# The first tiles of a streaming-encoder layer in another order: input tiles and weights by pairs, squares and the first gate's norm later

## The chip, the cores and the metric

The kernel runs on one core of a Trainium2 chip. The metric is the device time of one execution in microseconds (us). The engines named below are PE (TensorE: matmuls), ACT (ScalarE), DVE (VectorE), POOL (GpSimd) and SP (the engine that issues most transfers); each works through its own queue of instructions in a fixed order, and semaphores make one wait for another.

## What is computed

One layer on 528 tokens (512 of the input, 16 learned ones ahead of them) of width 1024: a half-weight SwiGLU feed-forward block, a mixing block of two head groups side by side, and a second half-weight SwiGLU block; each reads an RMS-normed stream and adds to it.

```python
def rmsnorm(x, g):
    y = xf * lax.rsqrt(jnp.mean(xf * xf, axis=-1, keepdims=True) + NORM_EPS)
    return (y * g.astype(jnp.float32)).astype(x.dtype)

def swiglu(x, w_gate, w_up, w_down):
    return (jax.nn.silu(x @ w_gate) * (x @ w_up)) @ w_down

#  h += 1/2 * SwiGLU(RMSNorm(h))                     feed-forward 1
#  n = RMSNorm(h); z = n @ W_in
#  h += concat(rwkv_out, attn_out) @ W_out           mixing: 8 RWKV heads, 8 windowed attention heads
#  h += 1/2 * SwiGLU(RMSNorm(h))                     feed-forward 2, then a final RMSNorm
```

The change touches the start of feed-forward 1. Everything else is the same work.

## The kernel before

**Numbers.** All is float32. A float32 operand is split into a rounded part (hi) and the rest (lo), both in the format that PE reads, and a product is made of three matmuls: weight hi by token hi (line 218), weight hi by token lo (line 219), and weight lo by token hi (line 200). 

**Tokens and units.** The tokens stand in two halves, half A (hf 0, 272 tokens) and half B (hf 1, 256). Weights come in units of 128 x 1024, eight blocks of 128 x 128 (k-tiles) each. Feed-forward 1 of half A runs unit by unit: gate of column block 0, up of block 0, gate of 1, up of 1 and so on; I number these units 0, 1, 2, 3. A unit is 16 hi matmuls and 8 lo matmuls in one PSUM bank; the tag `big` has four banks. `prep` (line 116) brings a unit: SP starts the transfer of `raw`, ACT casts it to `whi` (CAST, line 124), DVE subtracts to get `wlo` (line 127), each with three buffers. `drive` (line 133) keeps three units ahead of the one that is being multiplied.

**The start.** `consts0` (line 230) loads the small table `pv` of gains and runs 12 warm-up matmuls on a tile of ones (line 239). The first unit alone is brought in two halves of four k-tiles, each followed by `load_x`, four k-tiles of the input of half A. `boot[0]` = `start2(0)` then makes the norm of half A: squares on ACT (line 306), added up on DVE (line 310), summed over partitions by a matmul with ones (line 315), a square root on ACT (line 319, behind a load of its function table) and a reciprocal on DVE (line 320). Its result, `rs`, isn't needed for the operands of half A: `split` (line 331) makes them as input times gain (ACT, line 346: `nh`; DVE, line 347: `nl`), and `rs` comes in only behind the matmuls, in `up` (lines 381 to 404): gate bank times `rs` (DVE, line 396; this frees the gate's bank), silu (ACT, line 397, a function of another table), times `rs` (line 398), times the up bank (line 401; this frees the up bank), and the split of the product into hi and lo (lines 402 and 403). `ahead` makes all eight operands of half A at once. Half B's squares and norm (`start2(1)`) stand in the program behind step 22; its operands (`n1a`, `n1b`) do need `rs`.

**What sets the order.** The program is written step by step, but a scheduler that simulates the engines' time lines sets the order in each engine's queue. So an edit at the start can move rows far away from it. Names in the queues carry running numbers.

**Near the end of the mixing of half B** attention is interleaved with units of feed-forward 2 of half A. For each group of heads there are scores (line 907), a softmax on DVE and ACT (lines 913 to 923), transposes of it on PE into the banks `as` (lines 934 and 936), copies `pT` by ACT (lines 941 and 943), and products with the values (lines 946 and 949). There is one pair of `as` banks.

Of the kernel before, what the change touches and what calls it, by code (L numbers as in the profile page):

```python
# [7 lines left out]
F32 = mybir.dt.float32  # L8
R = mybir.dt.float32r
AF = mybir.ActivationFunctionType  # L10
ALU = mybir.AluOpType
# [14 lines left out]
T0 = (0, 272)  # L26
TT = (272, 256)
# [11 lines left out]
NK = D // 128  # L39
# [8 lines left out]
NPC = _n  # L48
# [7 lines left out]
UNIT = {}  # L56
# [14 lines left out]
class Prog:  # L71
# [44 lines left out]
    def prep(self, key, nk, first=False):  # L116
        raw = self.t(self.wp, [128, NK, 128], "raw", bufs=RAWB)
        hi = self.t(self.wp, [128, NK, 128], "whi", R, bufs=HIB)
        lo = self.t(self.wp, [128, NK, 128], "wlo", R, bufs=LOB)
        n = nk // 2 if first else nk  # L120
        for a in range(0, nk, n):
            self.nc.sync.dma_start(out=raw[:, a:a + n].rearrange("p k c -> p (k c)"),
                                   in_=self.io["w"][UNIT[key], :, a * 128:(a + n) * 128])
            self.A.copy(out=hi[:, a:a + n], in_=raw[:, a:a + n])  # L124
            if first:
                self.load_x(0, a)
        self.V.tensor_tensor(out=lo[:, 0:nk], in0=raw[:, 0:nk], in1=hi[:, 0:nk].bitcast(F32), op=ALU.subtract)  # L127
        return hi, lo

# [98 lines left out]


    def consts0(self):  # L230
        self.pv = self._ld("pv", [128, NPC])
# [55 lines left out]
        return self.dv[:, DC[name] + i:DC[name] + i + 1]  # L287


    def load_x(self, hf, d):  # L290
# [6 lines left out]
        self.nc.sync.dma_start(out=self.resv[:, d:d + 4], in_=self.io["xT"][:, d:d + 4, T0[hf]:T0[hf] + T])  # L297

    def sq_acc(self, hf, d, c0, end=False):

# [27 lines left out]

        return [self.t(self.np_, [128, 4, 2, T], f"n{hf}{x}", R) for x in "ab"]

    def split(self, hf, gain, c0, rs=None, ahead=True):

        T = TT[hf]
        parts = {}
        tiles = self.operands(hf, T)

        def part(d):
            if d in parts:
                return parts[d]
            np_ = tiles[d // 4][:, d % 4]  # L340
            nh, nl = np_[:, 0], np_[:, 1]
            n = self.res[hf, d]
            if rs is not None:
# [17 lines left out]
    def ffn_gu(self, f, g, hfs, ns):  # L361

        steps = []
        c0 = {hf: RO[hf] if f == 2 else 0 for hf in hfs}
        W = {hf: TT[hf] - c0[hf] for hf in hfs}
        j0, j1 = GROUPS[f][g]
        st = {}
        wide = f == 2 and tuple(hfs) == (1,)

        def gate(w):  # L370
            if wide:
                b = self.bank()
                self.wide3(b, w, ns[1], range(NK), 0, NK - 1)
                st["g"] = {1: self.both(b, self.t(self.fin, [128, 256], "gs", bufs=2))}
                return
            st["g"] = {hf: self.bank() for hf in hfs}
            self.mm3([st["g"][hf][:, :W[hf]] for hf in hfs], w, [ns[hf] for hf in hfs], NK)

        def up(j):
            def f_(w):  # L380
                pg, pu = st["g"], {hf: self.bank() for hf in hfs}
                if wide:
                    self.wide3(pu[1], w, ns[1], range(NK), 0, NK - 1)
                    pu = {1: self.both(pu[1], self.t(self.fin, [128, 256], "us", bufs=2))}
                else:
                    self.mm3([pu[hf][:, :W[hf]] for hf in hfs], w, [ns[hf] for hf in hfs], NK)
                for hf in hfs:
                    n = W[hf]
                    sl, hx = (self.sl[1], 1) if hf != hfs[0] else (self.sl[0], 0)
                    h = self.t(sl, [128, 2, TT[0]], f"h{hx}{j - j0}", R)  # L390
                    h = h.rearrange("p a t -> p (a t)")[:, 0:2 * n].rearrange("p (a t) -> p a t", a=2)
                    hh, hl = h[:, 0], h[:, 1]
                    s = self.t(self.tp, [128, TT[0]], "silu", bufs=2)
                    if f == 1 and hf == 0:
                        rs = self.rs1[hf]
                        self.V.tensor_tensor(out=s[:, :n], in0=pg[hf][:, :n], in1=rs[:, :n], op=ALU.mult)
                        self.A.activation(s[:, :n], s[:, :n], AF.Silu)
                        self.V.tensor_tensor(out=s[:, :n], in0=s[:, :n], in1=rs[:, :n], op=ALU.mult)
                    else:
                        self.A.activation(s[:, :n], pg[hf][:, :n], AF.Silu)  # L400
                    self.V.tensor_tensor(out=s[:, :n], in0=pu[hf][:, :n], in1=s[:, :n], op=ALU.mult)
                    self.A.copy(out=hh[:, :n], in_=s[:, :n])
                    self.V.tensor_tensor(out=hl[:, :n], in0=s[:, :n], in1=hh[:, :n].bitcast(F32), op=ALU.subtract)
                    self.hs[f, g, hf, j - j0] = h
# [553 lines left out]
def program(tc, io, out):  # L958
    with ExitStack() as ctx:
        pr = Prog(ctx, tc, io)  # L960
        n = {}
        A, B, AB = (0,), (1,), (0, 1)

        def renorm(gain, f):
            def last(hf):
                n[hf] = pr.norm(hf, gain, RO[hf] if f == 2 else 0)
            return last
# [21 lines left out]
        act = lambda fn: [(None, 0, 0, fn)]  # L989
# [7 lines left out]
        def pclose(name):  # L997
            pools.pop(name)[0].__exit__(None, None, None)

        def start2(hf):  # L1000
            def f():
                for d in range(NK):
                    pr.sq_acc(hf, d, 0)
                pr.rs1[hf] = pr.rstd(hf, 0, pr.mbank())
            return f

# [67 lines left out]
        fa = ffn(2, range(len(GROUPS[2])), A, final)  # L1074
        k = 10
# [6 lines left out]
        def lazy(hf):  # L1082
            made = []

            def n_(k):
                if not made:
                    made.append(pr.split(hf, "f1", 0, pr.rs1[hf] if hf else None, hf == 0))
                return made[0](k)
            return n_

        for hf in AB:
            n[hf] = lazy(hf)
        pr.drive(steps)
        pclose("fin")

# [111 lines left out]
```

## Time and profile before

| | us |
|---|---|
| median of three runs (1125.13 to 1130.59) | 1125.61 |
| the profiled execution | 1126.56 |
| its span, first to last instruction | 1124.5 |
| PE busy in the span | 1080.1 (96%) |
| DVE busy | 824.9 (73%) |
| ACT busy | 675.3 (60%) |
| POOL busy | 36.1 (3%) |

The profiled execution stands 0.95 us above the median of the runs, and 2.06 us of it lie outside the span. A line of the time line of an engine reads: start, duration, engine, line and operation, output <- inputs with shapes, number of instructions in the group, and in brackets how long the engine was idle just before and what released it. A line of a table by stretches reads: stretch, its length, then for each engine busy time and number of instructions, then PEclk, the share of full speed at which PE's clock was granted, the DMA share and GB/s.

### The profile page before, as it was taken

How to read it: one execution, taken by the hardware profiler on the slowest of the kernel's cores; microseconds unless marked ns; L12 is line 12 of the kernel's file. 1: busy time of each engine (PE TensorE's matmuls, PEld its weight loads, DVE VectorE, ACT ScalarE, POOL GpSimd, SP SyncE). 2: the span in 40 equal slices, each digit the busy share in tenths (PEclk: the TensorE clock that was granted, in tenths of full speed). 3: DMA queues.
4: the chain of work that ended last, by engine and by line, in shares of the span. 5: the costliest groups of instructions: out<-in, count | busy, mean ns of one | idle time of the engine just before them, and what ended most of it. 6: DMA issues, size and time to landing. Idle time of an engine off the chain costs nothing.

```text
span 1124.5 us, 23829 instructions
## 1 busy us (share of the span) xinstructions
PE 1080.1 (96%) x9621; PEld 1016.9 (90%) x9621; DVE 824.9 (73%) x1533; ACT 675.3 (60%) x1167; POOL 36.1 (3%) x91
## 2 busy tenths in 40 slices
PE   8999999999999997999999999998998999999996
PEld 7999999999899997988999898997887998888884
DVE  7866565777678995467799677996467588766666
ACT  7544444677666743587668685563577467545453
POOL 0000000022000000000002000000000000000000
PEclk8999999999999998999999999998999899999998
DMA  7556655655346546333555446547234456666561
GB/s 264 189 172 185 188 177 162 187 150 167 116 130 176 170 127 196 96 91 105 172 175 170 134 133 173 152 150 191 96 96 129 134 171 202 202 208 189 185 194 56
DMA packets 68721, 178.81 MB, mean 159 GB/s; under 512 B 21620, under 2 KB 26868, under 8 KB 68612
## 3 DMA queue, kind: packets, MB, share of 16 engines
q1 hardware_dynamic: 52384, 173.70, 50.3%
q10 hardware_dynamic: 16228, 3.61, 1.6%
q8 instruction: 75, 1.23, 0.4%
q14 instruction: 34, 0.28, 0.1%
HBM read 173.54 MB, written 3.74 MB: 158 GB/s over the span
## 4 chain that ended last, share of the span: by engine, by line
PE 72%; DVE 13%; ACT 7%; issue 3%; DMA 3%; ACTq 1%; DVEq 0%; SPq 0%
PE big L218 17%; PE big L219 16%; PE big L200 12%; PE big L206 11%; PE big L208 5%; DVE wlo L127 4%; PE big L227 4%; DVE tmp L731 3%; DVE rn L733 2%; ACT whi L124 2%; DMA zk<-d 1%; DMA d<-GT 1%; ACT s L920 1%; ACT L400 1%; DVE res L446 1%
## 5 line engine op out<-in xcount | busy, mean ns | idle before, releaser
L124 ACT CAST whi<-raw 128x1024 fp32r<-128x1024 f32 (+1 forms) x321 | 334.8, 1045 | 291.3 <-PE big L219 145.4
L127 DVE TENSOR_TENSOR wlo<-raw,whi 128x1024 fp32r<-128x1024 f32 x320 | 389.3, 1218 | 104.6 <-ACT whi L124 84.2
L219 PE MATMUL big<-h,whi 128*128 128x256 f32 (+1 forms) x528 | 135.4, 289 | 0.0
L218 PE MATMUL big<-h,whi 128*128 128x256 f32 (+1 forms) x528 | 131.9, 288 | 0.9 <-ACT silu L400 0.9
L218 PE MATMUL big<-n0a,whi 128*128 128x272 f32 (+1 forms) x464 | 122.3, 293 | 4.3 <-ACT n0a L346 2.3
L219 PE MATMUL big<-n0a,whi 128*128 128x272 f32 (+1 forms) x464 | 120.6, 289 | 0.4 <-DVE n0a L347 0.3
L218 PE MATMUL big<-n0b,whi 128*128 128x272 f32 (+1 forms) x464 | 120.4, 290 | 0.4 <-ACT n0b L346 0.3
L219 PE MATMUL big<-n0b,whi 128*128 128x272 f32 (+1 forms) x464 | 120.1, 289 | 0.4 <-DVE n0b L347 0.4
L219 PEld LDWEIGHTS big<-h,whi 128*128 128x128 f32 x528 | 101.1, 192 | 1.6 <-issue 1.3
L218 PEld LDWEIGHTS big<-h,whi 128*128 128x128 f32 x528 | 100.4, 193 | 1.3 <-ACT silu L400 1.1
L218 PEld LDWEIGHTS big<-n0a,whi 128*128 128x128 f32 x464 | 88.1, 190 | 6.8 <-ACT n0a L346 2.5
L219 PEld LDWEIGHTS big<-n0b,whi 128*128 128x128 f32 x464 | 88.1, 190 | 2.0 <-DVE n0b L347 0.7
L219 PEld LDWEIGHTS big<-n0a,whi 128*128 128x128 f32 x464 | 88.3, 191 | 1.6 <-DVE n0a L347 0.9
L218 PEld LDWEIGHTS big<-n0b,whi 128*128 128x128 f32 x464 | 88.0, 191 | 1.5 <-ACT n0b L346 0.9
L218 PE MATMUL big<-n1a,whi 128*128 128x256 f32 x288 | 76.2, 294 | 7.9 <-ACT whi L124 6.0
L227 PE MATMUL big<-h,wlo 128*128 128x256 f32 (+1 forms) x528 | 80.1, 286 | 0.3 <-DVE wlo L127 0.3
L200 PE MATMUL big<-n0a,wlo 128*128 128x272 f32 (+1 forms) x464 | 75.8, 285 | 0.0
L200 PE MATMUL big<-n0b,wlo 128*128 128x272 f32 (+1 forms) x464 | 75.7, 284 | 0.0
L219 PE MATMUL big<-n1a,whi 128*128 128x256 f32 x288 | 74.4, 288 | 0.0
L218 PE MATMUL big<-n1b,whi 128*128 128x256 f32 x288 | 73.9, 289 | 0.4 <-ACT n1b L953 0.4
L219 PE MATMUL big<-n1b,whi 128*128 128x256 f32 x288 | 73.9, 288 | 0.0
L227 PEld LDWEIGHTS big<-h,wlo 128*128 128x128 f32 x528 | 70.1, 188 | 2.2 <-issue 1.1
(313 smaller groups left out, 2216.1 us busy)
## 6 DMA issues: line engine op xcount, KB each, us to landing
raw<-w_in SPq DMA_DIRECT2D x319, 512.0 KB, 3.7
outT<-o SPq DMA_DIRECT2D x8, 256.0 KB, 2.6
res<-xT_in SPq DMA_DIRECT2D x2, 544.0 KB, 5.3
res<-xT_in SPq DMA_DIRECT2D x2, 512.0 KB, 9.0
d<-GT ACTq DMA_DIRECT2D x8, 80.0 KB, 4.2
zk<-d ACTq DMA_DIRECT2D x2, 320.0 KB, 4.1
d<-rn ACTq DMA_DIRECT2D x2, 320.0 KB, 3.9
GT<-d ACTq DMA_DIRECT2D x8, 80.0 KB, 5.1
```

The costliest lines, as they stand in the source:

```text
L124: self.A.copy(out=hi[:, a:a + n], in_=raw[:, a:a + n])
L127: self.V.tensor_tensor(out=lo[:, 0:nk], in0=raw[:, 0:nk], in1=hi[:, 0:nk].bitcast(F32), op=ALU.subtract)
L200: self.PE.matmul(o, lo[:, k], x(k)[:, 0], start=False, stop=(k == ks[-1]))
L206: self.PE.matmul(o, hi[:, i], x(k).rearrange("p a t -> p (a t)"), start=(k == first), stop=False)
L208: self.PE.matmul(o[:, 0:256], lo[:, i], x(k)[:, 0], start=False, stop=(k == last))
L218: self.PE.matmul(o, w, x[:, 0], start=first, stop=False)
L219: self.PE.matmul(o, w, x[:, 1], start=False, stop=False)
L227: self.PE.matmul(o, lo[:, i], x(k)[:, 0], start=False, stop=(k == nk - 1))
L400: self.A.activation(s[:, :n], pg[hf][:, :n], AF.Silu)
L446: self.V.scalar_tensor_tensor(out=r, in0=ps[hf][:, :W[hf]], scalar=0.5, in1=r, op0=ALU.mult, op1=ALU.add)
L731: V.tensor_tensor(out=m, in0=NT[:n2, 0:k, k].unsqueeze(1).broadcast_to([n2, k, k]), in1=TI[:n2, 0:k, 0:k], op=ALU.mult)
L733: V.tensor_reduce(out=TI[:n2, 0:k, k], in_=m, op=ALU.add, axis=mybir.AxisListType.X)
```

## The change

It has five parts.

1. **Order of the first transfers.** The input of half A is brought by two k-tiles instead of four. SP's order is: input 0 to 1, weights 0 to 3, `pv`, input 2 to 3, input 4 to 5, input 6 to 7, weights 4 to 7.
2. **The first cast by pairs.** ACT casts the first unit in four steps of two k-tiles (128 x 256); behind each step the operands of these two k-tiles are asked for (`first_x`).
3. **Two operands change their engine.** The hi part of k-tiles 6 and 7 of half A is made by DVE (a TENSOR_SCALAR, line 362 of the new kernel) instead of ACT (`turn`).
4. **Squares and norm of half A later.** The squares become a step behind unit 0, and `rs` of half A is made when the first gate's hidden product first asks for it.
5. **The first hidden product a unit later.** For column block 0 of half A the chain gate x `rs`, silu, x `rs`, x up is put off by one step (`self.late`): it is written behind the gate of block 1.

```diff
     def prep(self, key, nk, first=False):
-        n = nk // 2 if first else nk
+        n = 2 if first else nk
+        if first:
+            dma = lambda a, b: self.nc.sync.dma_start(out=raw[:, a:b]..., in_=self.io["w"][UNIT[key], :, a * 128:b * 128])
+            self.load_x(0, 0, 2)
+            dma(0, 4)
+            self.pv = self._ld("pv", [128, NPC])
+            for d in (2, 4, 6):
+                self.load_x(0, d, 2)
+            dma(4, 8)
+        else:
+            self.nc.sync.dma_start(out=raw[:, 0:n]..., in_=self.io["w"][UNIT[key], :, 0:n * 128])
         for a in range(0, nk, n):
-            self.nc.sync.dma_start(out=raw[:, a:a + n]..., in_=self.io["w"][UNIT[key], :, a * 128:(a + n) * 128])
             self.A.copy(out=hi[:, a:a + n], in_=raw[:, a:a + n])
             if first:
-                self.load_x(0, a)
+                for d in (a, a + 1):
+                    self.first_x(d)
...
-            self.A.activation(nh[:, c0:T], n[:, c0:T], AF.Copy, scale=self.P_(gain, d))
+            if d in turn:
+                self.V.tensor_scalar(out=nh[:, c0:T], in0=n[:, c0:T], scalar1=self.P_(gain, d), scalar2=0.0,
+                                     op0=ALU.mult, op1=ALU.add)
+            else:
+                self.A.activation(nh[:, c0:T], n[:, c0:T], AF.Copy, scale=self.P_(gain, d))
...
                     if f == 1 and hf == 0:
-                        rs = self.rs1[hf]
+                            if hf not in self.rs1:
+                                self.rs1[hf] = self.rstd(hf, 0, self.mbank())
+                            rs = self.rs1[hf]
...
+                if f == 1 and j == 0 and hfs == (0,):
+                    self.late.append((0, hidden))
+                else:
+                    hidden()
...
-        pr.boot = {0: start2(0), 2: load_b}
+        pr.boot = {2: load_b}
-        steps = fa[:22] + act(start2(1)) + fa[22:26]
+        steps = fa[:1] + act(lambda: squares(0)) + fa[1:22] + act(start2(1)) + fa[22:26]
...
-                    made.append(pr.split(hf, "f1", 0, pr.rs1[hf] if hf else None, hf == 0))
+                    made.append(pr.split(hf, "f1", 0, pr.rs1[hf] if hf else None, False, () if hf else (6, 7)))
```

In the queues the change shows at the following places. **SP, from its first transfer on**; `res` is the input, `raw` the weights. Before:

```order
1 L280 DMA pv<-pv_in 128x84
2 L122 DMA raw_100<-w_in 128x512
3 L297 DMA res_105<-xT_in 128x4x272
4 L122 DMA raw_100<-w_in 128x512
5 L297 DMA res_105<-xT_in 128x4x272
6 L122 DMA raw_138<-w_in 128x1024
```

Now:

```order
1 L308 DMA res_101<-xT_in 128x2x272
2 L123 DMA raw_98<-w_in 128x512
3 L291 DMA pv<-pv_in 128x84
4 L308 DMA res_101<-xT_in 128x2x272 x3
5 L123 DMA raw_98<-w_in 128x512
6 L132 DMA raw_133<-w_in 128x1024
```

The first input pair has moved to the front, and the second half of the first unit's weights behind all of the input; from row 6 on the queue is the same.

**ACT, where the square root of half A's norm stands.** `sq` are squares of half B, `whi_154` of before and `whi_149` of now are both the cast of unit 3, and `acc_5` / `acc_17` the square root of half A. Before:

```order
20 L306 ACTIVATE sq_938<-res_150 128x256
21 L306 ACTIVATE sq_941<-res_150 128x256
22 L124 CAST whi_154<-raw_153 128x1024
23 L306 ACTIVATE sq_944<-res_150 128x256
24 L319 ACT_TABLE_LOAD
25 L319 ACTIVATE acc_5_111<-mx_134,dv 128x272
26 L306 ACTIVATE sq_947<-res_150 128x256
27 L124 CAST whi_203<-raw_202 128x1024
```

Now:

```order
20 L317 ACTIVATE sq_942<-res_145 128x256
21 L317 ACTIVATE sq_945<-res_145 128x256
22 L330 ACT_TABLE_LOAD
23 L330 ACTIVATE acc_17_179<-mx_266,dv 128x272
24 L317 ACTIVATE sq_948<-res_145 128x256
25 L135 CAST whi_149<-raw_148 128x1024
26 L317 ACTIVATE sq_951<-res_145 128x256
27 L135 CAST whi_203<-raw_202 128x1024
```

The cast of unit 3 stood ahead of the table load and the square root, and stands behind them now. On PE the matmul that the square root waits for (line 315, now 326) stood behind the second matmul of unit 2, and stands behind the whole of unit 2 now, its lo part too. The first 12 hi matmuls of unit 5 now stand ahead of unit 4's lo part. Half B's sum, square root and reciprocal, which stood on PE between units 3 and 4, now stand about 20 units into the program, with a load of the square root's table and one of silu's around them on ACT.

**PE, near the end of half B's mixing**, at the attention of the last chunk's first group of heads; `big_1643` is a unit of feed-forward 2, `pT` the transposed softmax. Before:

```order
5242 L200 MATMUL big_1639_11094<-n0a_1084_7389,wlo_1622_10985 128x256 x4
5243 L200 MATMUL big_1639_11094<-n0b_1085_7390,wlo_1622_10985 128x256 x4
5244 L218 MATMUL big_1643_11125<-n0a_1084_7389,whi_1627_11021 128x256
5245 L219 MATMUL big_1643_11125<-n0a_1084_7389,whi_1627_11021 128x256
5246 L946 MATMUL as_1533_10367<-pT_1538_10407,VK_1511_10236 64x128
5247 L946 MATMUL as_1533_10367<-pT_1539_10410,VK_1511_10236 64x128
```

Now:

```order
5249 L212 MATMUL big_1643_11129<-n0a_1084_7393,wlo_1628_11026 128x256 x4
5250 L212 MATMUL big_1643_11129<-n0b_1085_7394,wlo_1628_11026 128x256 x4
5251 L960 MATMUL as_1533_10371<-ident_1540,s_1513_10244 81x128
5252 L962 MATMUL as_1533_10371<-ident_1540,s_1513_10244 128x128
5253 L960 MATMUL as_1533_10371<-ident_1540,s_1515_10249 81x128
5254 L962 MATMUL as_1533_10371<-ident_1540,s_1515_10249 128x128
5255 L972 MATMUL as_1533_10371<-pT_1538_10411,VK_1511_10240 64x128
5256 L972 MATMUL as_1533_10371<-pT_1539_10414,VK_1511_10240 64x128
```

The transposes and the products of this group of heads stood apart, with a unit's matmuls between them, and stand in one row now, behind the end of `big_1643`. Between the two places (from some 130 us to the mixing of half B, and behind its end) the queues' orders are the same.

## Rows read from the trace of the kernel before

**Rows 1.** The page, part 1: busy us, share of the span, instructions.
```profile
PE 1080.1 (96%) x9621; PEld 1016.9 (90%) x9621; DVE 824.9 (73%) x1533; ACT 675.3 (60%) x1167; POOL 36.1 (3%) x91
```

**Rows 2.** Table by stretches: busy time of the engines, PEclk, DMA share, GB/s.
```profile
5.48:7.77 2.29, 0.01 (x1) 0.00 (x0) 0.64 (x2) 1.53 (x5) 0.00 (x0) 0.97 0.95 317
7.77:18.39 10.62, 9.91 (x40) 8.79 (x40) 10.39 (x24) 8.89 (x20) 0.00 (x0) 0.52 1.07 370
18.39:27.00 8.61, 8.24 (x64) 7.79 (x63) 7.43 (x11) 7.12 (x10) 0.00 (x0) 1.00 0.53 168
27.00:56.00 29.00, 29.00 (x234) 29.00 (x234) 25.91 (x49) 17.38 (x30) 0.00 (x0) 1.00 0.60 197
95.00:130.00 35.00, 35.00 (x283) 35.00 (x282) 22.57 (x36) 17.27 (x24) 0.00 (x0) 1.00 0.60 182
871.20:878.00 6.80, 5.58 (x29) 4.66 (x28) 0.29 (x1) 1.33 (x7) 0.00 (x0) 0.50 0.05 19
```

**Rows 3.** Time line of PE in the first 30 us.
```profile
7.78 0.59 PE L218 MATMUL big<-n0a,whi 128*128 128x272 f32 x1 [2.29 <-ACT n0a L346]
...
19.75 0.62 PE L315 MATMUL mx<-acc,ones 128*128 128x272 f32 x2
...
22.94 0.29 PE L218 MATMUL big<-n0a,whi 128*128 128x272 f32 x1
...
25.93 0.59 PE L315 MATMUL mx<-acc,ones 128*128 128x256 f32 x2
26.90 0.36 PE L218 MATMUL big<-n0a,whi 128*128 128x272 f32 x1 [0.37 <-DVE silu L396]
...
29.96 0.29 PE L218 MATMUL big<-n0a,whi 128*128 128x272 f32 x1
```

**Rows 4.** Time line of ACT in the first 22 us.
```profile
4.01 0.62 ACT L124 CAST whi<-raw 128x512 fp32r<-128x512 f32 x1 [1.99 <-DMA raw<-w_in]
6.24 0.43 ACT L306 ACTIVATE acc<-res 128x272 f32<-128x272 f32 x1 [1.62 <-DMA res<-xT_in]
...
7.22 1.75 ACT L346 ACTIVATE n0a<-res,pv 128x272 fp32r<-128x272 f32 x4
...
18.82 1.04 ACT L124 CAST whi<-raw 128x1024 fp32r<-128x1024 f32 x1
19.77 0.41 ACT L306 ACTIVATE sq<-res 128x256 f32<-128x256 f32 x1
20.19 1.28 ACT L319 ACT_TABLE_LOAD   x1
21.48 0.49 ACT L319 ACTIVATE acc<-mx,dv 128x272 f32<-128x272 f32 x1
```

**Rows 5.** Time line of DVE from 17 to 27 us.
```profile
17.50 0.64 DVE L263 TENSOR_SCALAR tabm<-tabm,pv 128x8 f32<-128x8 f32 x4
...
22.00 1.85 DVE L320 RECIPROCAL acc<-acc 128x272 f32<-128x272 f32 x1 [0.55 <-ACT acc L319]
23.77 0.36 DVE L310 TENSOR_TENSOR acc<-acc,sq 128x256 f32<-128x256 f32 x1
24.05 2.35 DVE L127 TENSOR_TENSOR wlo<-raw,whi 128x1024 fp32r<-128x1024 f32 x2
26.32 0.78 DVE L396 TENSOR_TENSOR silu<-big,acc 128x272 f32<-128x272 f32 x2
```

**Rows 6.** Time line of PE, 834 to 880 us, at attention's waits.
```profile
843.89 0.44 PE L946 MATMUL as<-pT,VK 81*64 81x128 f32 x4 [0.69 <-ACT pT L943]
858.05 0.34 PE L934 MATMUL as<-ident,s 128*81 128x128 f32 x1 [0.76 <-ACT VK L932]
870.96 0.34 PE L934 MATMUL as<-ident,s 128*81 128x128 f32 x1 [2.08 <-ACT s L923]
872.89 0.69 PE L946 MATMUL as<-pT,VK 81*64 81x128 f32 x4 [0.85 <-ACT pT L943]
```

More of the change, by code (lines that the diff above doesn't have):

```diff
@@ L119, in prep @@
         lo = self.t(self.wp, [128, NK, 128], "wlo", R, bufs=LOB)
-        n = nk // 2 if first else nk
+        n = 2 if first else nk
+        if first:
+            dma = lambda a, b: self.nc.sync.dma_start(out=raw[:, a:b].rearrange("p k c -> p (k c)"),
+                                                      in_=self.io["w"][UNIT[key], :, a * 128:b * 128])
+            self.load_x(0, 0, 2)
[5 more added lines that the diff above has]
+        else:
+            self.nc.sync.dma_start(out=raw[:, 0:n].rearrange("p k c -> p (k c)"),
+                                   in_=self.io["w"][UNIT[key], :, 0:n * 128])
         for a in range(0, nk, n):
-            self.nc.sync.dma_start(out=raw[:, a:a + n].rearrange("p k c -> p (k c)"),
-                                   in_=self.io["w"][UNIT[key], :, a * 128:(a + n) * 128])
             self.A.copy(out=hi[:, a:a + n], in_=raw[:, a:a + n])
             if first:
-                self.load_x(0, a)
+                for d in (a, a + 1):
+                    self.first_x(d)
         self.V.tensor_tensor(out=lo[:, 0:nk], in0=raw[:, 0:nk], in1=hi[:, 0:nk].bitcast(F32), op=ALU.subtract)
@@ L230, in consts0 @@
     def consts0(self):
-        self.pv = self._ld("pv", [128, NPC])
         self.ones = self.cst.tile([128, 128], F32, name="ones")
@@ L287, in D_, with load_x @@
         return self.dv[:, DC[name] + i:DC[name] + i + 1]
-    def load_x(self, hf, d):
+    def load_x(self, hf, d, n=4):
         T = TT[hf]
@@ L296, in load_x @@
             self.resv = r
-        self.nc.sync.dma_start(out=self.resv[:, d:d + 4], in_=self.io["xT"][:, d:d + 4, T0[hf]:T0[hf] + T])
+        self.nc.sync.dma_start(out=self.resv[:, d:d + n], in_=self.io["xT"][:, d:d + n, T0[hf]:T0[hf] + T])
     def sq_acc(self, hf, d, c0, end=False):
@@ L329, in operands, with first_x, split @@
         return [self.t(self.np_, [128, 4, 2, T], f"n{hf}{x}", R) for x in "ab"]
-    def split(self, hf, gain, c0, rs=None, ahead=True):
+    def first_x(self, d):
+        self.n0(d)
+    def split(self, hf, gain, c0, rs=None, ahead=True, turn=()):
         T = TT[hf]
@@ L386, in f_ @@
                     self.mm3([pu[hf][:, :W[hf]] for hf in hfs], w, [ns[hf] for hf in hfs], NK)
[L387 to L394, printed above, removed]
-                        rs = self.rs1[hf]
[L396 to L404, printed above, removed]
@@ new lines, in hidden @@
+                def hidden():
+                    for hf in hfs:
+                        n = W[hf]
+                        sl, hx = (self.sl[1], 1) if hf != hfs[0] else (self.sl[0], 0)
+                        h = self.t(sl, [128, 2, TT[0]], f"h{hx}{j - j0}", R)
+                        h = h.rearrange("p a t -> p (a t)")[:, 0:2 * n].rearrange("p (a t) -> p a t", a=2)
+                        hh, hl = h[:, 0], h[:, 1]
+                        s = self.t(self.tp, [128, TT[0]], "silu", bufs=2)
+                        if f == 1 and hf == 0:
+                            if hf not in self.rs1:
+                                self.rs1[hf] = self.rstd(hf, 0, self.mbank())
+                            rs = self.rs1[hf]
+                            self.V.tensor_tensor(out=s[:, :n], in0=pg[hf][:, :n], in1=rs[:, :n], op=ALU.mult)
+                            self.A.activation(s[:, :n], s[:, :n], AF.Silu)
+                            self.V.tensor_tensor(out=s[:, :n], in0=s[:, :n], in1=rs[:, :n], op=ALU.mult)
+                        else:
+                            self.A.activation(s[:, :n], pg[hf][:, :n], AF.Silu)
+                        self.V.tensor_tensor(out=s[:, :n], in0=pu[hf][:, :n], in1=s[:, :n], op=ALU.mult)
+                        self.A.copy(out=hh[:, :n], in_=s[:, :n])
+                        self.V.tensor_tensor(out=hl[:, :n], in0=s[:, :n], in1=hh[:, :n].bitcast(F32), op=ALU.subtract)
+                        self.hs[f, g, hf, j - j0] = h
@@ L405, in up @@
+                if f == 1 and j == 0 and hfs == (0,):
+                    self.late.append((0, hidden))
+                else:
+                    hidden()
             return f_
@@ L998, in pclose, with squares @@
             pools.pop(name)[0].__exit__(None, None, None)
+        def squares(hf):
+            for d in range(NK):
+                pr.sq_acc(hf, d, 0)
         def start2(hf):
             def f():
-                for d in range(NK):
-                    pr.sq_acc(hf, d, 0)
+                squares(hf)
                 pr.rs1[hf] = pr.rstd(hf, 0, pr.mbank())
@@ L1092, in program @@
             n[hf] = lazy(hf)
+        pr.n0 = n[0]
         pr.drive(steps)
```

## The prediction

> **What bounds the kernel now.** I first read the busy shares on the page. PE is busy for 96% of the span, and neither DVE nor ACT is near that [rows 1]. So only two things can move the time: moments in which PE waits, and stretches in which its matmuls run at the lower of its two clock levels. Next the table by stretches: PE is idle from 5.48 to 7.77, works at a granted clock of 0.52 (about the 1.2 GHz level) until 18.39 and at 1.00 (2.4 GHz) afterwards, and from 27 to 56 us it has no gap at all [rows 2]. So whatever this change wins at the start must be won before about 30 us; later on it only shifts the work. Third, PE's time line, to see the waits by name: 2.29 us for the first hi operand at 7.78, and 0.37 us at 26.90 for the multiplication by `rs` that frees the first gate's bank [rows 3]. That second wait is the end of a chain which I read on ACT and DVE: table load at 20.19, square root at 21.48, reciprocal at 22.00, two `wlo`, line 396 at 26.32, unit 4 at 26.90 [rows 3 to 5]. This chain, not the arrival of data, sets when unit 4 starts. The cost of the low clock follows from the table: 40 matmuls in 9.91 us are 0.25 us each at the low level, and 64 in 8.24 are 0.13 at the high one [rows 2]; counted by starts, unit 3's 24 matmuls fill 22.94 to 25.93, 0.125 each [rows 3].
>
> **The change, part by part.**
>
> *First transfers.* Before, the first weights have landed at 4.0 and the first four input tiles at 6.24 [rows 4], after 298 and 842 KB in SP's order. By the same bytes in the new order the first input pair (272 KB) lands at about 4, weights 0 to 3 (528 KB) at 4.9, `pv` at 5.1, input 2 to 3 at 6.2, and at the 317 to 370 GB/s of the stretches [rows 2] input 4 to 5 at 7.1, 6 to 7 at 7.9 and weights 4 to 7 at 8.7. From there the bytes that have come are those of before.
>
> *First unit.* ACT then casts 128 x 256 twice (0.62 for 128 x 512 [rows 4], so some 0.35 each) from 4.9 and makes the first hi operand (0.44 each, four in 1.75 [rows 4]) by 6.0. The first matmul starts at about 6.1 instead of 7.78: 1.7 us earlier. Moving two hi operands to DVE takes two times 0.44 off ACT; the trace has no such operation on DVE, but anything between nothing and 0.5 us (the lo operand is of that size) is covered, because the second half of the weights arrives only at 8.7. The hi part of unit 0 ends at about 11.1, and nothing after it waits for data until unit 3.
>
> *The norm of half A.* Here the gain meets another order. The matmul that sums the squares stood two matmuls into unit 2; now it stands behind units 0, 1 and 2. From 11.1 these are 56 matmuls. At 0.125 that is 7.0 us, so it runs at 18.1 to 18.7; each us in which the clock is low past 11.1 adds about 0.45. On ACT the table load comes earlier: a cast (1.04) and a square (0.41) no longer stand ahead of it, and DVE's additions no longer stand behind four small instructions (0.64) [rows 4, 5]. From 20.19 that leaves about 18.2, and the square root can't start before 19.5. So it starts at the later of 19.5 and the sum's end: 19.5 with the clock up throughout, 20.3 with it low to about 14.5, 21.9 with it low to 17.9; before it was 21.48.
>
> *What waits behind it.* The cast of unit 3 now stands behind the square root. The root (0.4 until the next one starts), a square (0.33) and the cast (1.04) put unit 3 at the root plus 1.84: 21.3, 22.2 or 23.7, against 22.94 [rows 3]. Unit 4 follows 3.0 later, without its old wait, since reciprocal, one `wlo` and the multiplication end by the root plus 4.2. Then comes a new wait: 12 hi matmuls of unit 5 stand ahead of unit 4's lo part, and unit 5 needs the first up bank, which is freed late in DVE's queue. From the root: 0.5 to the reciprocal, 1.77 for it, 0.34 for an addition, 1.13 for `wlo`, 0.70 for two multiplications, 0.34 for an addition, 2.3 for two `wlo`, 0.70 and 0.43 for the next three, all by the spacing of [rows 5]: 8.2. So unit 5 starts at 27.7, 28.6 or 30.1. Behind it 32 matmuls (4.0 us) stand before unit 6: 31.7, 32.6 or 34.1.
>
> *Against before.* Unit 6 of before starts 24 matmuls behind 29.96 [rows 3], at 32.95. It had the sum for half B behind it by then, some 0.5 us [rows 3], which the new order owes until later. So the comparison is with 32.5: a gain of 0.8 with the clock up, a loss of 0.1 with it low to 14.5, a loss of 1.6 with it low as long as before. **Most of the 1.7 us won at the first matmul is spent again waiting for the norm**, since the sum of the squares and unit 3's cast have moved back in their queues.
>
> *Half B's norm.* It moves to about 95 to 130 us and takes two more table loads there (1.28 each [rows 4]) and the reciprocal. PE is busy for all of that stretch while ACT works 17.27 and DVE 22.57 of 35 us [rows 2]; three units of weights lie ahead. I cost it at 0; if the units ahead were used up, it would be at most the two loads, 2.6.
>
> *Near the end of half B's mixing.* The waits of before are 0.69 and 0.85 for `pT`, 0.76 for `VK`, and 2.08 for the softmax [rows 6], together 4.4. The new order puts transposes and products of one group of heads in a row, so a wait of some 0.85 for `pT` arises there, and about 0.4 for the freed bank behind it; 0.69 and 0.76 have other matmuls ahead of them now. I take the sum as -0.3, with +-1.5 either way. The clock falls to 0.50 from 871 to 878 after these waits [rows 2]; if it fell twice, 29 matmuls at the low price would cost another 3.5.
>
> *Clock at the start.* Before, PE's idle 2.29 us ended with the clock low [rows 2]. Now the idle time is 0.6, but the first unit trickles: eight matmuls from 6.1 to 8.2, then a wait to 9.1 for the second half of the weights. I choose the middle case, a shorter low stretch. The Trainium skill, TensorE: Matmul & The Clock Gate, section "HAM oscillation — how this bites in real kernels", says that where the work on a k-tile is shorter than the wait for the next one's data, PE falls back to the low clock at each of them; bringing tiles by pairs makes just such a start. By that rule the third case holds. No row here has PE fed by pairs.
>
> **Sum.** On the profiled execution's own time: 1126.56 + 0.1 (start) - 0.3 (mixing) = 1126.4. The median of the runs lies 0.95 lower, so 1125.4, which I put at 1125.2 since the first case pulls a little further than the second.
>
> **Rivals.**
>
> *A, the early start comes through* (chance 0.22). The clock stays up from 6 us on, or the square root isn't late, and the whole of the 0.8 to 1.7 us stays won; with 1 off the mixing, 1122.9 to 1124. For it: the idle time ahead of the first matmul falls from 2.29 to 0.6. Against: the table load on ACT caps the gain at 0.8 by the rows.
>
> *B, slower: the norm's chain* (chance 0.25). The clock is low as long as before, the sum of the squares runs at 21.2, the square root at 21.9, and unit 3's cast stands behind it: +1.6, and with +1 in the mixing 1127.2 to 1128.2. It decides from where the sum runs later than 19.6, which is a low clock past about 14.4. The skill's rule above leads here.
>
> *C, the change doesn't do what it says* (chance 0.10). Smaller input transfers and weights behind them land later than the bytes say; the first matmul then starts at 7 or later and unit 0 ends as before: 1125.6 to 1127.
>
> *D, the other place decides* (chance 0.08, half of it to either side). The new order near 840 to 878 us opens or closes a wait of 2 us or moves the low clock by a stretch: 1121.5 or 1129.5.
>
> **How the numbers follow.** The forecast, little changed at 1125.2, has a chance of 0.35. The range goes from A's better end, 1122.9, to B's upper one, 1128.2, each widened by the 0.9 that lies between two executions of the same kernel (the profiled one and the median): 1122.0 to 1129.1. It leaves out D's ends. About 0.5% (5.6 us) is what a measurement of this kernel can tell from no change; to reach that faster, start and mixing would both have to give more than their whole waits of about 7 us: 0.04. To be slower by it, B and D would have to come together and more: 0.04. So 0.92 for the same.
>
> **What would show it.** PE's first matmul at about 6.1; the granted clock from 7 to 18 us; the sum's matmul (line 326) at 18 to 21; unit 3 released by ACT's cast behind the square root; a wait of over 1 us at the first matmul of unit 5, released by line 423; no wait of PE at 95 to 130; and attention's waits together near 4 us. It is wrong if unit 6 starts before 31 us or after 35, or if units that I take to be unmoved between 130 and 834 take another time.

## The result: slower, and the time went at the end of half B's mixing

The changed kernel takes 1134.26 us (median of 7 runs, 1129.92 to 1137.8), the kernel before 1128.24 in the runs beside it (1125.13 to 1131.75). The ratio is 1.0054, with an interval from 1.0034 to 1.0074: 4 to 8 us slower. I had forecast 1125.2 and a range up to 1129.1. The profiled execution of the changed kernel takes 1136.02 us, its span is 1133.0.

To find where the two part, I take one row per unit: the start of the DVE subtraction that makes `wlo`. There are 320 of them in both kernels, in the same order. I number them from 0 and subtract the start before from the start after.

```
wlo of unit    start before    start after    after - before
     40           129.25          129.32         +0.07
    108           361.33          361.77         +0.44
    133           447.62          448.37         +0.75
    150           537.65          541.42         +3.77
    228           821.10          825.43         +4.34
    241           883.79          892.05         +8.26
    315          1092.13         1100.39         +8.26
```

So the start, which the change is about, is a draw. Some 3 us come between 447 and 538 us, in a stretch where the order of all queues is the same in both kernels; and 3.9 us come between 821 and 884 us, at the end of half B's mixing.

**The start came out at the forecast figure.** The table by stretches of the kernel after, with busy times, number of instructions, granted clock, DMA share and GB/s:

```profile
0.00:9.39 9.39, 6.94 (x32) 6.29 (x32) 5.41 (x30) 6.04 (x14) 0.61 (x7) 1.00 0.76 231
9.39:16.20 6.81, 6.51 (x26) 6.00 (x27) 6.60 (x12) 4.70 (x10) 0.00 (x0) 0.50 1.08 370
16.20:30.00 13.80, 11.98 (x94) 11.55 (x94) 10.49 (x21) 9.90 (x16) 0.00 (x0) 1.00 0.55 183
95.00:130.00 35.00, 35.00 (x283) 35.00 (x282) 25.60 (x45) 18.58 (x28) 0.00 (x0) 1.00 0.60 184
872.96:886.61 13.65, 10.73 (x48) 8.88 (x49) 1.99 (x14) 4.96 (x14) 0.00 (x0) 0.50 0.13 40
```

The low clock at the start lasts 6.8 us instead of about 10 (rows 1 and 2 here answer to the second row of [rows 2]). Half B's norm, now between 95 and 130, leaves PE busy for all of the 35 us. The last row shows twice the low stretch that [rows 2] had at 871. The time line of PE after, at the places that answer to [rows 3]:

```profile
6.08 0.37 PE L230 MATMUL big<-n0a,whi 128*128 128x272 f32 x1
...
9.68 0.59 PE L230 MATMUL big<-n0b,whi 128*128 128x272 f32 x1 [1.55 <-ACT whi L135]
...
12.29 0.43 PE L230 MATMUL big<-n0a,whi 128*128 128x272 f32 x1
...
21.04 0.62 PE L326 MATMUL mx<-acc,ones 128*128 128x272 f32 x2
23.47 0.39 PE L230 MATMUL big<-n0a,whi 128*128 128x272 f32 x1 [1.81 <-ACT whi L135]
...
28.61 0.29 PE L230 MATMUL big<-n0a,whi 128*128 128x272 f32 x1
...
32.59 0.29 PE L230 MATMUL big<-n0a,whi 128*128 128x272 f32 x1
```

The rows are the first matmul, the wait for the second half of the first unit's weights, the start of unit 1, the sum of the squares, and the starts of units 3, 5 and 6. And ACT after, where the square root stands (to [rows 4]):

```profile
18.41 1.28 ACT L330 ACT_TABLE_LOAD   x1
21.70 0.49 ACT L330 ACTIVATE acc<-mx,dv 128x272 f32<-128x272 f32 x1 [2.00 <-PE mx L326]
...
22.39 1.03 ACT L135 CAST whi<-raw 128x1024 fp32r<-128x1024 f32 x1
```

The table is loaded 1.8 us earlier, then ACT stands idle for 2.00 us until PE has summed the squares, and unit 3's cast waits behind it. At unit 3, which starts at 23.47 (before: 22.94), PE's 1.7 us are gone.

**The mixing did not.** The time line of PE after, around the last two groups of heads (to [rows 6]):

```profile
847.27 0.68 PE L869 MATMUL mx<-UV,BT 64*64 64x64 f32 x16 [1.27 <-ACT grs L904]
...
868.82 0.63 PE L212 MATMUL big<-n0b,wlo 128*128 128x256 f32 x4
869.28 0.27 PE L960 MATMUL as<-ident,s 128*81 128x128 f32 x1
...
872.05 0.44 PE L972 MATMUL as<-pT,VK 81*64 81x128 f32 x4 [2.17 <-ACT pT L969]
...
873.08 1.01 PE L230 MATMUL big<-n1b,whi 128*128 128x256 f32 x3 [0.36 <-ACT n1b L979]
874.02 1.07 PE L933 MATMUL as<-KC,Q 64*128 64x209 f32 x4
...
878.90 0.51 PE L960 MATMUL as<-ident,s 128*81 128x128 f32 x1 [1.59 <-ACT s L949]
...
880.89 0.69 PE L972 MATMUL as<-pT,VK 81*64 81x128 f32 x4 [0.85 <-ACT pT L969]
```

The product of the last-but-one group waits 2.17 us for `pT`. The scores of the last group need the bank that this product frees, so they run at 874.02, with nine unit matmuls between them and their transposes. In the kernel before the last lo matmuls of `big_1643` and the same scores, with ten matmuls behind them, ran here:

```profile
866.07 0.63 PE L200 MATMUL big<-n0b,wlo 128*128 128x256 f32 x4
...
866.87 0.62 PE L907 MATMUL as<-KC,Q 64*128 64x209 f32 x4
```

At the last lo matmuls of unit `big_1643` the kernel after is 2.75 us late (868.82 against 866.07), at the scores 7.15. About 1 us of the 4.4 between is work, the transposes and products that the kernel before had done earlier; the rest is waiting and the low clock. The reason for the 2.17 is on ACT after:

```profile
868.74 1.28 ACT L422 ACT_TABLE_LOAD   x1
870.03 0.38 ACT L422 ACTIVATE silu<-big 128x256 f32<-128x256 f32 x1
870.31 1.04 ACT L135 CAST whi<-raw 128x1024 fp32r<-128x1024 f32 x1
871.25 0.26 ACT L967 COPY pT<-as 81x128 f32<-81x128 f32 x1
...
871.72 0.28 ACT L969 COPY pT<-as 128x128 f32<-128x128 f32 x1
```

PE's transposes are done by 869.9, but a table load, a silu and a cast of a unit stand ahead of the four copies in ACT's queue.

How much of the 3.9 us PE stands idle can be counted. The table by stretches from unit 228 to unit 241, of the kernel before and of the one after:

```profile
821.10:883.79 62.69, 57.49 (x668) 52.29 (x668) 39.83 (x95) 44.26 (x93) 0.69 (x2) 0.95 0.35 102
```

```profile
825.43:892.05 66.62, 60.00 (x668) 54.55 (x668) 39.67 (x95) 46.05 (x94) 0.48 (x2) 0.90 0.31 96
```

PE's idle time grows from 5.2 to 6.6 us, by 1.4. The other 2.5 us are busy time of the same number of instructions, at a mean granted clock of 0.90 instead of 0.95. Some of these slower matmuls run beside a chain that PE would else have waited for, so the 2.5 are not what a higher clock would give back.

### The profile page after: what moved, and what is told of

Same layout as the page of the kernel before. It is cut to its first block, busy times and chain, and to the rows that moved or that the text cites. A ratio compares the mean times of both kernels' runs of the same rounds, so it can differ in the third digit from the quotient of the medians.

```text
span 1133.0 us, 23831 instructions
## 1 busy us (share of the span) xinstructions
PE 1087.0 (96%) x9621; PEld 1023.3 (90%) x9621; DVE 826.1 (73%) x1535; ACT 679.2 (60%) x1170; POOL 34.4 (3%) x91
## 4 chain that ended last, share of the span: by engine, by line
PE 72%; DVE 14%; ACT 6%; issue 3%; DMA 3%; ACTq 1%; SPq 0%; DVEq 0%
PE big L230 17%; PE big L231 16%; PE big L212 12%; PE big L218 11%; PE big L220 5%; DVE wlo L139 5%; PE big L239 4%; DVE tmp L757 3%; DVE rn L759 2%; ACT whi L135 2%; DMA zk<-d 1%; DMA raw<-w_in 1%; DMA d<-GT 1%; ACTq L771 1%; DMA d<-rn 1%
## 5 line engine op out<-in xcount | busy, mean ns | idle before, releaser
L230 PE MATMUL big<-n1b,whi 128*128 128x256 f32 x288 | 75.3, 294 | 0.7 <-ACT n1b L979 0.7
L231 PE MATMUL big<-n1b,whi 128*128 128x256 f32 x288 | 75.5, 293 | 0.0
```

What stands on the lines that cost most here:

```text
L230: self.PE.matmul(o, w, x[:, 0], start=first, stop=False)
L231: self.PE.matmul(o, w, x[:, 1], start=False, stop=False)
```

## The experiments

Two things can be read from the queues alone. Undoing parts 4 and 5 (squares, norm and hidden product later) moves no row at all on any engine: the scheduler takes what is ready, and where these steps are written doesn't count. And taking part 3 away (two operands on DVE) brings back the old order at the end of half B's mixing and of half B's norm.

The theories: M, the loss is the new order of the mixing's end and the start is a draw; S, the start costs it; H, half B's norm and its two table loads cost it; W, within M, it is waits and not the clock.

**Part 3 undone.**

```diff
-  made.append(pr.split(..., False, () if hf else (6, 7)))
+  made.append(pr.split(..., False, ()))
```

> The changed kernel, but the two hi operands of k-tiles 6 and 7 are made by ACT again. Its queues keep the new transfers and casts by pairs at the start and have the old order at the end of half B's mixing and for half B's norm. Theory M (the mixing's new order costs the time, the start is neutral): within 2 us of the kernel before, so 4 to 6 us faster than the changed one; units 60 to 230 start within 1 us of before except where the clock falls. Rival S (the start costs it: new transfers shift everything or the phase in which the clock falls): 4 to 6 us slower than before, like the changed kernel.

Ratio to before 1.0047 (1.0025 to 1.0069), so against M's forecast. But the place differs: unit 40 is 2.80 us late already, and from unit 228 to 241 nothing is lost (+4.09 to +4.07). The undone part changed the order of the start too, in a way that I had not taken into account: half B's sum, square root and reciprocal came back to the start, and the reciprocal now stands ahead of the multiplication that frees the first gate's bank. DVE, and PE, of this run:

```profile
24.87 1.74 DVE L331 RECIPROCAL acc<-acc 128x256 f32<-128x256 f32 x1
26.53 1.16 DVE L139 TENSOR_TENSOR wlo<-raw,whi 128x1024 fp32r<-128x1024 f32 x1
27.61 0.77 DVE L418 TENSOR_TENSOR silu<-big,acc 128x272 f32<-128x272 f32 x2
```

```profile
28.18 0.36 PE L230 MATMUL big<-n0a,whi 128*128 128x272 f32 x1 [3.95 <-DVE silu L418]
```

A wait of 3.95 us at unit 4, with a low-clock stretch behind it. So 2.8 of the some 5 us that this run loses lie at its start; as a test of M it only says that the old mixing order loses nothing.

**Old transfers, new mixing order.**

```diff
+            self.pv = self._ld("pv", [128, NPC])
+            dma(0, 4)
+            self.load_x(0, 0, 4)
+            dma(4, 8)
+            self.load_x(0, 4, 4)
```

(in place of the seven starts of the changed kernel)

> The changed kernel with SP's old order of the first transfers (pv, weights 0 to 3, input 0 to 3, weights 4 to 7, input 4 to 7); casts by pairs and two operands on DVE stay. Its start is nearly that of before (about a dozen PE rows of the first 90 stand otherwise), its mixing end has the new order. Theory M: 4 to 6 us slower than before, with a wait of about 2 us for pT behind the last-but-one transposes and over 10 us of low clock around 870 to 890. Rival S: within 2 us of before.

Ratio 1.0057 (1.0035 to 1.0080). Unit 40 is 0.53 late, and units 228 to 241 lose 3.9 us, as in the changed kernel. The waits of PE from 833 to 888 us are those of the changed kernel to the tenth:

```profile
PE as L971 <- ACT pT L968: 3.0, 2, 2.2
PE as L959 <- ACT s L948: 1.6, 1, 1.6
PE mx L868 <- ACT grs L903: 1.3, 1, 1.3
```

The columns are: total us, times, longest. With the old transfers and nearly the old start, the loss is there. Against S.

**Parts 4 and 5 undone**, the queues row for row the same:

```diff
-        pr.boot = {2: load_b}
+        pr.boot = {0: start2(0), 2: load_b}
-        steps = fa[:1] + act(lambda: squares(0)) + fa[1:22] + ...
+        steps = fa[:22] + ...
-                if f == 1 and j == 0 and hfs == (0,):
+                if False:
```

> The changed kernel with parts 4 and 5 undone: squares and norm of half A stand in the program where they stood, the first hidden product isn't put off. Its queues are row for row those of the changed kernel. So every theory expects the changed kernel's time, 4 to 8 us over before; a result apart from that would show how much of a difference is chance. If the two low stretches at 460 and 525 us of the changed kernel's profile are chance, they need not be in this one.

Ratio 1.0047 (1.0030 to 1.0064), the changed kernel's within the interval. In its profile units 228 to 241 lose 3.8 us, and the 3 us between units 133 and 150 are missing (-0.42 at unit 133, -0.41 at 150). So the mixing's loss comes with the order, and those 3 us don't.

**PE kept busy in the waits.**

```diff
+                if c == 7:
+                    for _ in range(3 if mp2 else 9):
+                        PE.matmul(bo[:, 384:512], self.ones, rows[1][0][:, 0:128], start=True, stop=True)
```

> The changed kernel with extra matmuls on a tile of ones in the waits for pT of the last chunk: 9 behind the transposes of the first group of heads, 3 behind those of the second, into unused columns of the bank; their results are not used. PE is then busy in the wait of 2.2 us. Theory M with the clock as its larger half: the low stretch from 873 us is 6.8 instead of 13.7 us long and 2.5 to 3.5 us come back, so 1 to 3 us over before. Rival W (the waits alone cost it): no gain, 4 to 7 us over before.

Ratio 1.0039 (1.0024 to 1.0055). The low stretch behind the waits is half as long, as forecast for the clock:

```profile
865.30:875.64 10.34, 6.58 (x54) 5.40 (x53) 3.69 (x17) 6.45 (x16) 0.00 (x0) 1.00 0.34 103
875.64:882.50 6.86, 5.65 (x30) 4.95 (x30) 0.29 (x1) 1.02 (x5) 0.00 (x0) 0.50 0.00 0
```

but units 228 to 241 still lose 4.2 us. PE's time line says why: the copies of `pT` had to wait for the extra matmuls (each of the nine is two records), so the wait came after them.

```profile
865.34 0.27 PE L960 MATMUL as<-ident,s 128*81 128x128 f32 x1
...
865.78 2.17 PE L965 MATMUL as<-s,ones 128*128 128x128 f32 x18
868.80 0.44 PE L975 MATMUL as<-pT,VK 81*64 81x128 f32 x4 [0.85 <-ACT pT L972]
...
874.82 0.34 PE L960 MATMUL as<-ident,s 128*81 128x128 f32 x1 [2.54 <-ACT s L949]
...
877.63 0.69 PE L975 MATMUL as<-pT,VK 81*64 81x128 f32 x4 [0.85 <-ACT pT L972]
```

What the clock gave, the longer chains took. From the transposes to the products of a group PE needed 2.77 and 1.99 us in the changed kernel (869.28 to 872.05, 878.90 to 880.89) and 3.46 and 2.81 here (865.34 to 868.80, 874.82 to 877.63): 1.5 us more. Units 228 to 241 lose only 0.3 us more than in the changed kernel, so by this estimate the shorter low stretch gave back 1.2 us and not 2.5 to 3.5. The time agrees with W's forecast, but W isn't shown, since the run made the chains longer too; what it speaks against is the clock as the larger half.

**The changed kernel with another order of the mixing only.** One line gives the attention of half B a priority in the scheduler; all up to about 790 us stays row for row.

```diff
             def begin_at():
+                PRIO["attn"] = 60 if hf else 0
```

> The changed kernel with one line added: from the attention of half B on, the scheduler is given a higher priority (60 instead of 0) for attention. Start and everything to about 790 us stand row for row as in the changed kernel; at the end of half B's mixing the last scores now have 48 matmuls of the units between them and their transposes, instead of 9. Theory M (the loss lies in how much other work stands behind the last scores): the waits for s and pT of the last two groups of heads fall from 4.6 to under 2 us, the low stretch around 870 is gone or half as long, and the time falls by 4 to 7 us against the changed kernel, to within 2 us of the kernel before. Rival S (the start, or half B's later norm, costs it): no change against the changed kernel, 4 to 6 us over before.

Ratio 0.9999 (0.9981 to 1.0017): with the changed start, the changed transfers and half B's later norm all in place, the loss is gone. Units 228 to 241 gain 0.6 us, and the low stretch behind the waits is half as long as in the changed kernel (877.1 to 883.9, 6.8 us). The waits of PE at attention from 834 to 890 us (the one for `pT` is the last group's; the product of the last-but-one group doesn't wait):

```profile
PE as L960 <- ACT s L949: 0.8, 1, 0.8
...
PE as L972 <- ACT pT L969: 0.2, 1, 0.2
```

**The same with priority 100**, 23 matmuls behind the last scores:

> As the run before it, with priority 100: 23 matmuls stand between the last scores and their transposes. Theory M: between the two, waits of 2 to 3.5 us there, 2 to 5 us faster than the changed kernel. Rival S: no change.

Ratio 0.9988 (0.9976 to 1.0000), some 7 us faster than the changed kernel by the two ratios, more than forecast. Units 228 to 241 gain 0.1 us. The waits for `s` and `pT`, 2.6 us together, are in the forecast range, yet the time is no worse than with 48 matmuls: the dose does not show in the time. It could not be the whole of M anyway, since ten matmuls stood behind the last scores in the kernel before and nine in the changed one. What both runs with a priority lack, and the changed kernel has, is the wait of 2.17 for `pT` in the last-but-one group.

```profile
PE as L960 <- ACT s L949: 1.8, 1, 1.8
PE as L960 <- ACT VK L958: 1.4, 1, 1.4
PE as L972 <- ACT pT L969: 0.8, 1, 0.8
```

**The kernel before with 45 matmuls behind the last scores** (`PRIO["attn"] = 140 if hf else 0`):

> The kernel before with the priority of half B's attention at 140: its start and all to about 790 us as before, 45 matmuls behind the last scores instead of 10. Theory M: the wait of 2.08 for s goes, that of 0.85 too or nearly, and the low stretch of 871 to 878 shrinks: 2 to 5 us faster than before, unless the chain of the other head group waits in turn. Rival: no change, because other waits of the same length come at the places from which work was taken.

Ratio 1.0009 (0.9994 to 1.0024): no gain, as the rival said. The wait for `s` fell from 2.08 to 0.9 us, but the low stretch behind it is still 6.8 us long (877.1 to 883.9), and a new wait of 3.0 stands at 821.9 us, where the priority has changed the order too, with 3.4 us of low clock from 822.5 on:

```profile
PE as L928 <- ACT BT L806: 3.0, 1, 3.0
```

**The kernel before with part 5 alone**, its queues row for row those of before:

> The kernel before with part 5 alone (the first hidden product written a step later). Its queues are row for row those of before. Every theory: the time of before within 1.5 us. Its profile shows whether low stretches near 460 and 525 us, which before's profile lacks and the changed kernel's has, can come with the order of before: if yes they are chance, if they are tied to the changed start they stay away.

Ratio 0.9993 (0.9979 to 1.0007). The table by stretches of the kernel before, and then of this one, at the two places in question:

```profile
458.19:461.60 3.41, 3.41 (x36) 3.08 (x35) 0.66 (x2) 2.00 (x5) 0.00 (x0) 1.00 0.15 59
523.05:526.46 3.41, 3.41 (x65) 3.34 (x65) 2.99 (x7) 1.41 (x7) 0.00 (x0) 1.00 0.43 118
```

```profile
458.19:461.60 3.41, 3.41 (x25) 3.29 (x25) 0.42 (x1) 1.27 (x4) 0.00 (x0) 0.50 0.05 20
523.05:526.46 3.41, 3.41 (x38) 3.19 (x39) 2.32 (x4) 1.15 (x3) 0.00 (x0) 0.50 0.32 70
```

The same instructions in the same order, once at 1.00 and once at 0.50; between units 133 and 150 this execution loses 3.0 us against the other. So the 3 us of the changed kernel's profile at this place are chance of the execution and not the change.

**Two trials more.** First, the kernel with priority 100 and `WARM = 16`:

> The run with 23 matmuls behind the last scores (priority 100), with 16 warm-up matmuls instead of 12, so that PE has work until about 6.4 us, some 0.3 us past the arrival of the first operands. Theory M with the start nearly neutral: the low stretch at the start (3.4 to 6.8 us long in the runs so far) may get shorter, worth up to 1 us at unit 3; the time is 0 to 3 us below before. Rival: the later first matmul costs as much as the clock gives back, and the time is that of the run with priority 100 alone, 0 to 1.5 us below before.

Ratio 0.9986 (0.9973 to 0.9999), 1127.19 against 1129.17 us in the medians: the only version whose interval lies below before, by 1.6 us as the ratio has it, and 0.7% below the changed kernel if the two ratios are divided. The low stretch at the start is 3.4 us long, no shorter than with 12 (3.4 to 6.8), so what the warm-up does is not shown; it isn't told apart from priority 100 alone.

Second, part 3 alone on the kernel before:

> The kernel before with part 3 alone: the two hi operands of k-tiles 6 and 7 on DVE, old transfers, old casts. The scheduler again moves half B's norm to 95 to 130 us and reorders the mixing's end, but into a third order: 15 matmuls behind the last scores, transposes and products of the last-but-one group not in one row. Theory M (what counts is how the last two groups of heads are placed): within 2 us of before, although half B's norm stands where the changed kernel has it. Rival H (half B's later norm, with two more table loads, costs the time): 3 to 6 us over before.

Ratio 1.0022 (1.0010 to 1.0035), 2.5 us over before: between the two forecasts. PE waits for nothing between 40 and 140 us, where half B's norm now stands, so H is out. Unit 40 is 0.75 late from the start, and units 228 to 241 lose 1.0, at the last group's softmax, in spite of the 15 matmuls:

```profile
869.19 0.62 PE L911 MATMUL as<-KC,Q 64*128 64x209 f32 x4
875.35 0.50 PE L938 MATMUL as<-ident,s 128*81 128x128 f32 x1 [3.54 <-ACT s L927]
```

All kernels at a glance, by the start of `wlo` against before:

```
kernel                       unit 40   unit 228   unit 241   228 to 241   order of mixing's end
changed                       +0.07      +4.34      +8.26       +3.9       new
old transfers                 +0.53      +3.43      +7.37       +3.9       new
parts 4, 5 undone             -0.66      -0.25      +3.51       +3.8       new
PE kept busy                  -0.51      +0.41      +4.61       +4.2       new, extra matmuls
part 3 undone                 +2.80      +4.09      +4.07        0.0       old
before's twin                 -0.18      +2.71      +2.91       +0.2       old
changed, priority 60          -1.22      +5.60      +5.04       -0.6       third
changed, priority 100         -0.68      +3.81      +3.69       -0.1       fourth
priority 100, 16 warm-ups     -0.37      +0.41      +0.30       -0.1       fourth
before, priority 140          -0.09      +3.11      +4.89       +1.8       fifth
part 3 alone                  +0.75      +2.92      +3.91       +1.0       sixth
```

Up to unit 40 the changed start is between 0.1 us late and 1.2 us early. From unit 40 to 228 every kernel loses between 0.4 and 6.8 us against the one execution of before that was profiled, its own twin 2.9. The last step alone follows the order: four kernels with the new order lose 3.8 to 4.2 us, two with the old one 0.0 and 0.2.

## Why the prediction was wrong

**Right in its number: the start.** The first matmul was forecast at 6.1 and came at 6.08; the square root's chain eats the gain, as worked out: table load early, root held by the sum on PE (2.00 us), unit 3's cast behind it, unit 3 at 23.47 (forecast 21.3 to 23.7; the three parts of the 1.84 from root to unit 3 add up to 1.77, and 1.77 came). Unit 6 was forecast at 32.6 in the case that I chose, and started at 32.59; the net of the start, +0.1, was +0.07.

**Two details of it were wrong and cancelled, so the hit is luck.** The sum ran at 21.04, not at about 19.6: the hi part of unit 0 ended at 12.29 and not at 11.1, since its second half began at 9.68 instead of 9.1 and ran at the low clock, and the clock stayed low to 16.2 and not to 14.5. With the root at 21.70 my own terms (8.2 to unit 5, 4.0 to unit 6) give unit 6 at 33.9, a loss of 1.4. But the wait at unit 5 for the first up bank didn't come: unit 5 began at 28.61 in one row with unit 4, while line 423, which frees that bank, ran at 29.40. Only the two gates' banks had been freed by then (line 418, both in one go at 25.39), so unit 5 had taken the second gate's. I had taken for granted that banks come round in the order in which they were filled. On DVE after:

```profile
25.39 0.78 DVE L418 TENSOR_TENSOR silu<-big,acc 128x272 f32<-128x272 f32 x2
...
29.40 0.43 DVE L423 TENSOR_TENSOR silu<-big,silu 128x272 f32<-128x272 f32 x1
```

**The clock at the start.** It fell to its lower level at 9.39, within the wait of 1.55 for the second pair of casts, later and for a shorter time than before (6.8 us against 10.2). In four more executions with this start, and in the one with 16 warm-ups, the low stretch was 3.4 us long; the old start had 10.2 us in two executions (before and its twin) and 6.8 in a third (priority 140), so one execution alone doesn't give this length. Of the Trainium skill's rule (TensorE: Matmul & The Clock Gate, "HAM oscillation — how this bites in real kernels"), one fall of the clock at a wait for data is borne out here. A low clock as long as before, which I had drawn from it, is not.

**Right: half B's norm at 0.** PE was busy for all of 95 to 130 us.

**Wrong: the term for the mixing's end.** I wrote -0.3 with +-1.5. It measured +3.9. I priced the new wait for `pT` at 0.85, the length that such a wait has when ACT is free [rows 6], and left out what stands on ACT ahead of the copies: a table load, a silu and a cast, 2.7 us, and the wait was 2.17. A wait of 1.27 for `grs`, a tile of the other head group (0.38 before), wasn't in the term; the waits of 0.69 and 0.76 did go, as forecast. I also took the last group's chain as unchanged. It starts when the previous group's product frees the only pair of banks, and with that product behind the end of `big_1643` the chain starts there too; from scores to transposes it was 4.09 us long in the kernel before (866.87 to 870.96) and 4.88 now. The wait that is left uncovered at its end fell from 2.08 to 1.59, since the scores and the nine matmuls beside it ran at the low clock and cover more of the chain. And the clock: the waits of 2.17 and 1.59 came one upon the other, and the low stretch lasted 13.65 us instead of 6.8, with 48 matmuls in it instead of 29 [rows 2]; by the estimate from the run with PE kept busy, its second half is worth some 1.2 of the 3.9 us.

I had a rival for the place, D, with 2 us or one more low stretch, at 1129.5. That is 3.9 over the 1125.6 that I started from, and 3.9 is what the place measured; but I gave this side a chance of 0.04 and left it out of the range.

**Wrong as well: the base and the spread.** Of the 9.1 us between the forecast and 1134.26, 2.6 have nothing to do with the change. I started from the median of three runs, 1125.61; with seven it was 1128.24. And I widened the range by 0.9 for what lies between two executions of one kernel, while 35 runs of the kernel before spread over 8.1 us. One of my signs of being wrong, that units between 130 and 834 take another time, came true for that reason: the twin of before shows the same 3 us between units 133 and 150.

Parts 4 and 5, which the section on the change names as what puts the norm and the first hidden product later, move no row; part 3 turns the scheduler's order, at half B's norm and at the mixing's end.

**What stays open.** The ratios of the four kernels with the new order stand for 4 to 6 us (1.0039 to 1.0057), the profiles place 3.8 to 4.2 of it. The rest, 0 to 2 us, lies in no place that I can name; since executions with the same queues differ by up to 4 us between units 40 and 228 (+4.3 in the changed kernel, +0.4 with parts 4 and 5 undone), it may be chance. How the 3.9 us divide between waits and clock is an estimate only (some 1.2 for the clock), since the extra matmuls delayed the copies. That the table load, the silu and the cast ahead of the copies make the wait of 2.17 is read from the trace; no run moves them alone. Whether the 16 warm-ups add anything to priority 100 wasn't settled either.

## What to carry to other kernels

Where a scheduler sets the order, read the whole difference of the queues first, and price each place where it moved rows like an edit of its own; an edit at the start that comes out even there can turn an order 800 us later that loses four. To price a product that moved, list what stands ahead of its operands on the other engine's queue, and look for the resource (here one pair of PSUM banks) that lets the next chain begin only when it is done. A wait in a trace is only the uncovered end of a chain: count what covers it before you take it as given.

## What the hardware showed beyond this

The same instructions in the same queues ran once at the upper and once at the lower clock in two stretches, around 458 and 523 us, within which PE has records without a break in both executions; each such stretch cost 1.5 us. In both executions PE had waited 1.9 us shortly ahead of the second stretch (to 521.26 in the kernel before), and not at all in the 20 us ahead of the first. In the 35 runs of one comparison the kernel before lay between 1125.01 and 1133.1 us. A single profile therefore can't place a difference of 3 us between two kernels; the comparison by places with three or four kernels of the same order could.
